# Surveying and combining the down projection's weights during the up projection, and making its token sums in two passes

## The chip, the cores and the metric

The kernel runs on one core of one Trainium2 chip. TensorE (PE) multiplies matrices; VectorE (DVE), ScalarE (ACT) and GpSimd (POOL) do the arithmetic around it; SyncE (SP) issues nearly all transfers between the chip's main memory and the on-chip buffer. The engines run at the same time, each through its own list of instructions in order, and wait for one another by semaphores.

The metric is the device time of one execution in microseconds (us), as the median of several runs. One further execution was recorded by the hardware profiler; all profile rows come from it.

## The reference

`reference()` is one layer of an encoder on x of 1024 tokens by 1024 features, in float32:

```python
h = layer_norm(x, ln_in_w, ln_in_b)
h = layer_norm(A * h + hybrid_mixer(h, ...), ln1_w, ln1_b)   # mLSTM heads and neighbourhood attention
h = layer_norm(A * h + memory_xattn(h, mem, ...), ln2_w, ln2_b)
h = layer_norm(A * h + conv_ffn(h, ...), ln3_w, ln3_b)

def conv_ffn(x, w_up, b_up, w_dw, b_dw, w_down, b_down):
    h = x @ w_up + b_up
    h = depthwise_conv3(h, w_dw) + b_dw        # along the positions
    g, u = jnp.split(h, 2, axis=-1)
    y = jax.nn.gelu(g, approximate=False) * u
    return y @ w_down + b_down
```

A is 2 to the power 0.25. The inner width is 2816, so `w_up` is 1024 x 5632 and `w_down` 2816 x 1024. The mixer begins with one combined projection of the normed x.

## The kernel before

**Arithmetic.** A float32 operand is scaled by a power of two and split into two float16 parts, a high one on ACT and a low one on DVE (`split16`, lines L204 and L205). A product then takes three matmuls (`mm3`, L225 to L227), typically of 128x512 results. To scale an operand its largest magnitude must be bounded first. That is a "survey": ACT takes absolute values and accumulates a sum for each partition.

**Seven products.** The large projections use a Strassen-like scheme. Both operands are cut into 2 x 2 blocks, and seven block products replace eight. On the weight side this needs sums of blocks, T1 to T4; on the token side S1 to S4.

**Stages.** (1) Input norm, keys and values of the memory tokens, token-major projections. (2) The feature-major part of the mixer's projection in four units u = 0..3 (`units_gen`, bank `cu` in the profile). `cu_prep` loads a unit's weights in two transfers (L459, tile `wraw`), surveys them (L311), splits them (L204, L205) and lets POOL make four sums (L477 to L480), which are split too. ACT and DVE take the results out of the banks (L506, L504). (3) mLSTM, neighbourhood attention, output projection, cross attention. (4) The up projection: a loop over v = 0..21, in which PE multiplies unit v, POOL makes the four sums of unit v + 2 (L1600 to L1603), ACT and DVE do the convolution and the gate of unit v - 1 (L1741 to L1750), and the activation y of each unit is stored to main memory. (5) The down projection. Blocks 0 to 15 of the inner width take the seven products in the order A11·B11, A12·B21, A22·T4, n2·T2, n1·T1, s3·T3, n4·B22; blocks 16 to 21 are multiplied directly. The layer norm ends it.

**The parts that the change touches.** While stage 2 runs, `td_gen` (L983 to L1008) goes through the first 16 blocks of `w_down` in 16 pieces of 512 KB. For each it loads the piece (L991, tile `draw`, three buffers), surveys it on ACT (L999, tile `djunk`), makes four 128x256 sums in place on POOL (L1001 to L1004) and stores the four combinations T1 to T4 to main memory (L1006, tensor `td`). The loop over stage 2's yields takes a step of `td_gen` at most of its turns, and an anchor (`taken`) keeps each survey behind the latest bank that ACT emptied. The other six blocks of `w_down` are surveyed one at a time in the up loop at v = 2..7 (`survey_down`, tile `sv`, two buffers, L1786).

In stage 5 `b_form` loads a weight form in two halves of 1 MB and splits it, and `a_sums(i)` loads two blocks of y (2 x 512 KB) and makes both sums that two products need: two on DVE (L1819, L1820), two on POOL (L1821, L1822), then two splits of 128x1024. The first (index m = 0, tiles SX1 and SX2 in `dx` and `zw` products) feeds n1 and n2, the second (m = 1) feeds s3 and n4. All these loads rotate through three 1 MB buffers, named `two` and `ur` in the profile.

**What sets the order.** A scheduler orders each engine's instructions from the program; `tc.issue_after` anchors hold one behind another. Every SP transfer waits in SP's list until its buffer is free, and holds up the transfers behind it.

## Time and profile before

| | us |
|---|---|
| runs | 1484.5, 1489.22, 1488.21 |
| median | 1488.21 |
| the profiled execution's own time | 1485.82 |
| its span in the profile | 1483.4 |
| PE busy | 1420.7 (96%) |
| DVE busy | 1074.7 (72%) |
| ACT busy | 850.9 (57%) |
| POOL busy | 655.3 (44%) |

The mean granted TensorE clock was 0.985 of full speed. The span is the time between the first and the last recorded instruction; the execution's own time is 2.4 us longer. Busy time counts arithmetic only. With PE busy for 96% of the span, the time can fall only where PE stands still, runs at a lower clock, or gets fewer matmuls; the stretches where that happens are found by cutting the span into windows and by asking what ended PE's waits.

Views used below: the waits (engine, what it was about to run, whom it waited for: total us, times, longest us); the windows (start and end, length, then busy us and instruction count of PE, of its weight loads, of DVE, ACT and POOL, then the granted clock, the busy share of the transfer engines, GB/s); the timeline (start us, duration us, engine, line, operation, output and input, count, and in brackets the idle time before it and what ended it); and a tile's own instructions (nanoseconds minimum/median/maximum, then first and last start).

### The profile page before, as it was taken

Reading aid. Unit: us, or ns where it says so; the run is one execution under the profiler, and the core shown is the slowest. Engines: PE = TensorE matmul, PEld = TensorE weight load, DVE = VectorE, ACT = ScalarE, POOL = GpSimd, SP = SyncE. Lnnn points to the kernel's source line nnn. Section 1 sums busy time; section 2 is a strip of 40 time slices with the busy share of each in tenths; the row PEclk is TensorE's granted clock in tenths of the full one; section 3 lists DMA queues with packets and bytes.
Section 4 is the critical chain, followed back from the end, with each engine's and each line's share of the span. In section 5 each row is a group of like instructions: output and inputs, shape, how many; then the busy total and the mean of one; then the engine's idle time right before and its main releaser. Section 6 shows DMA issues by size and latency. Waiting matters only on the chain. (4 is left out here: it accounts for less than half of the span.)

```text
span 1483.4 us, 21399 instructions
## 1 busy us (share of the span) xinstructions
PE 1420.7 (96%) x7864; PEld 835.2 (56%) x7864; DVE 1074.7 (72%) x1956; ACT 850.9 (57%) x1399; POOL 655.3 (44%) x528
## 2 busy tenths in 40 slices
PE   7999899969999999999999999999999999998997
PEld 6898777435676677675444444444444444443443
DVE  7767866733667777858756878888888778898346
ACT  4775464766564467723455667777667767645201
POOL 4444338755432675416302334454444420055494
PEclk9999999989999999999999999999999999999999
DMA  9764654467654563464452423322222225766322
GB/s 328 272 240 139 198 185 158 154 207 234 179 149 121 169 225 122 161 236 123 87 118 66 150 80 129 141 100 85 86 86 85 85 86 180 273 235 238 110 72 99
DMA packets 133040, 229.56 MB, mean 155 GB/s; under 512 B 41028, under 2 KB 86340, under 8 KB 128199
## 3 DMA queue, kind: packets, MB, share of 16 engines
q1 hardware_dynamic: 132640, 227.44, 46.1%
q8 instruction: 61, 1.00, 0.3%
q0 software_dynamic: 144, 0.49, 0.2%
q14 instruction: 45, 0.36, 0.1%
q10 hardware_dynamic: 150, 0.27, 0.0%
HBM read 166.73 MB, written 53.54 MB: 148 GB/s over the span
## 5 line engine op out<-in xcount | busy, mean ns | idle before, releaser
L225 PEld LDWEIGHTS <-whi 128*128 128x128 f16 x574 | 56.5, 98 | 68.8 <-ACT whi L204 8.7
L1742 DVE SCALAR_TENSOR_TENSOR cbuf<-C,wdw,cbuf 128x1024 f32<-128x1024 f32 x44 | 65.2, 1483 | 36.9 <-ACT cbuf L1741 36.7
L226 PEld LDWEIGHTS <-whi 128*128 128x128 f16 x574 | 56.5, 98 | 62.5 <-issue 7.2
L227 PEld LDWEIGHTS <-wlo 128*128 128x128 f16 x574 | 56.4, 98 | 61.7 <-DVE wlo L205 2.0
L1600 POOL TENSOR_TENSOR wraw<-two 128x512 f32<-128x512 f32 x15 | 30.1, 2008 | 123.0 <-issue 121.8
L205 DVE SCALAR_TENSOR_TENSOR wlo<-wraw,us,whi 128x1024 f16<-128x1024 f32 (+1 forms) x48 | 62.4, 1320 | 25.6 <-ACT whi L204 25.5
L1741 ACT ACTIVATE cbuf<-C,bdw,wdw 128x1024 f32<-128x1024 f32 x44 | 54.4, 1238 | 43.1 <-DVE C L1779 42.5
L245 POOL TENSOR_TENSOR lnrs<-lnrs,mhalf 128x1 f32<-128x1 f32 x32 | 21.2, 663 | 125.7 <-DVE lnrs L244 117.1
L1743 DVE SCALAR_TENSOR_TENSOR cbuf<-C,wdw,cbuf 128x1024 f32<-128x1024 f32 x44 | 71.3, 1621 | 1.1
L204 ACT ACTIVATE whi<-wraw,us 128x1024 f16<-128x1024 f32 (+1 forms) x48 | 51.1, 1103 | 10.8 <-DVE us L177 10.3
L225 PE MATMUL tk<-whi,Bo 128*128 128x256 f16 (+1 forms) x192 | 53.7, 280 | 1.6 <-DVE stage L205 1.6
L226 PE MATMUL tk<-wlo,Be 128*128 128x256 f16 (+1 forms) x192 | 52.6, 274 | 1.5 <-DVE wlo L205 1.5
L226 PE MATMUL tk<-wlo,Bo 128*128 128x256 f16 (+1 forms) x192 | 53.7, 280 | 0.0
L227 PE MATMUL tk<-whi,Bo 128*128 128x256 f16 (+1 forms) x192 | 53.7, 280 | 0.0
L225 PE MATMUL tk<-whi,Be 128*128 128x256 f16 (+1 forms) x192 | 52.6, 274 | 0.8 <-ACT whi L204 0.5
L227 PE MATMUL tk<-whi,Be 128*128 128x256 f16 (+1 forms) x192 | 52.6, 274 | 0.0
L225 PE MATMUL S<-kq,h1T 128*128 128x512 f16 x128 | 48.6, 379 | 0.0
L226 PE MATMUL S<-kq,h1T 128*128 128x512 f16 x128 | 48.5, 379 | 0.0
L227 PE MATMUL S<-kq,h1T 128*128 128x512 f16 x128 | 48.5, 379 | 0.0
L1821 POOL TENSOR_TENSOR wraw<-two 128x512 f32<-128x512 f32 x2 | 3.8, 1885 | 97.2 <-DMA two<-y 92.5
L1270 ACT ACTIVATE P<-P,mn 128x256 f32<-128x256 f32 (+1 forms) x64 | 35.7, 558 | 16.0 <-DVE mn L1268 14.9
L255 ACT ACTIVATE D<-D,lnrs 128x1024 f32<-128x1024 f32 x5 | 6.2, 1241 | 66.2 <-DVE lnrs L254 66.2
(654 smaller groups left out, 5159.3 us busy)
## 6 DMA issues: line engine op xcount, KB each, us to landing
two<-in_w_up_dram SPq DMA_DIRECT2D x15, 1024.0 KB
y<-cbuf SPq DMA_DIRECT2D x22, 512.0 KB
draw<-in_w_dn_dram SPq DMA_DIRECT2D x16, 512.0 KB
td<-draw SPq DMA_DIRECT2D x16, 512.0 KB
ur<-in_w_up_dram SPq DMA_DIRECT2D x7, 1024.0 KB
two<-y SPq DMA_DIRECT2D x6, 1024.0 KB
two<-y SPq DMA_DIRECT2D x12, 512.0 KB
wraw<-in_w_tok_dram SPq DMA_DIRECT2D x10, 512.0 KB
```

Source lines behind the costliest of these rows:

```text
L204: A.activation(hi, src, AF.Copy, scale=s)
L205: return V.scalar_tensor_tensor(lo, src, s, hi, op0=OP.mult, op1=OP.subtract)
L225: T.matmul(ps, lh, rh, start=first, stop=False, skip_group_check=skip)
L226: T.matmul(ps, lh, rl, start=False, stop=False, skip_group_check=skip)
L227: return T.matmul(ps, ll, rh, start=False, stop=last, skip_group_check=skip)
L245: G.tensor_tensor(rs[:, 0:1], rs[:, 0:1], mhalf[:, 0:1], OP.pow)
L255: A.activation(r, r, AF.Identity, scale=rs[:, 0:1], bias=rs[:, 1:2])
L1270: A.activation(P[:, :nk], P[:, :nk], AF.Exp, scale=-1.0, bias=mn[:, 0:1], accum_out=mn[:, 1:2])
L1600: G.tensor_tensor(S1, A21, A22, OP.add)
L1741: A.activation(c, C[:, 1:SEQ + 1], AF.Identity, scale=wdw[:, 1, j:j + 1], bias=bdw[:, j:j + 1])
L1742: V.scalar_tensor_tensor(c, C[:, 0:SEQ], wdw[:, 0, j:j + 1], c, op0=OP.mult, op1=OP.add)
L1743: V.scalar_tensor_tensor(c, C[:, 2:SEQ + 2], wdw[:, 2, j:j + 1], c, op0=OP.mult, op1=OP.add)
```

## The change

`td_gen` and its pool are removed, and with it all that stood in stage 2 for it. `survey_down` now covers all 22 blocks, from v = 2 to v = 19, one per unit and two at v = 4, 8, 12 and 16. For the first 16 it also makes the four sums on POOL, in place in `sv`, and POOL itself issues the store to `td`. The survey writes its absolute values to a scratch tile, so that `sv` keeps the weights.

The weights are laid out anew in main memory: each of 16 pieces holds the four 256-column blocks that are combined, 4 KB per partition, and `td` has the same shape. `b_form` reads every form by one access pattern of 1 KB runs.

`a_sums(m, i)` makes only one of the two sums: two additions on DVE for m = 0, three for m = 1, then one split. Each y block is so loaded twice. POOL's sixteen additions go. All eight steps with m = 0 precede the T1 form; those with m = 1 are spread behind T3 and the n1·T1 product. The final norm's vectors are loaded and scaled later.

```diff
-    td_d = dscratch("td", [4, 128, 8 * 512])
+    td_d = dscratch("td", [16, 128, D])
...
-            dp = cm.enter_context(tc.tile_pool(name="dp", bufs=1, reuse_waits="tile"))
-            def td_gen():
-
-                junk = dp.tile([128, 1024], BF, name="djunk")
-                raws = {}
-
-                def load(n):
-                    if n < 16:
-                        raws[n] = dp.tile([128, 4, 256], F32, name="draw", tag="draw", bufs=3)
-                        S.dma_start(raws[n], I["w_dn"][n // 2].rearrange("p (b c) -> p b c", b=4)[
-                            :, :, n % 2 * 256:n % 2 * 256 + 256])
-
-                load(0)
-                load(1)
-                for n in range(16):
-                    raw = raws.pop(n)
-                    with tc.issue_after(taken[0].ins):
-                        A.activation(junk, raw.rearrange("p b c -> p (b c)"), AF.Abs, accum_out=sums[:, NFF + n:NFF + n + 1])
-                    B11, B12, B21, B22 = (raw[:, i] for i in range(4))
-                    G.tensor_tensor(B11, B11, B12, OP.add)
-                    G.tensor_tensor(B12, B12, B22, OP.add)
-                    G.tensor_tensor(B22, B22, B11, OP.add)
-                    G.tensor_tensor(B21, B21, B22, OP.add)
-                    o = n // 2 * 512 + n % 2 * 256
-                    S.dma_start(td_d[:, :, o:o + 256].rearrange("n p c -> p n c"), raw)
-                    load(n + 2)
-                    yield
-            bg, td = back_gen(), td_gen()
+            bg = back_gen()
             for n, _ in enumerate(units_gen(cu0)):
-                if n % 7 % 2 == 0:
-                    next(td, None)
                 if n >= 14:
                     next(bg, None)
-            run(td)
             run(bg)
             prep(0)
             gram(0)
...
                 t = sv[i % 2]
                 with tc.issue_after(loaded.ins):
-                    S.dma_start(t, I["w_dr"][i // 2, :, i % 2 * 1024:i % 2 * 1024 + 1024])
-                A.activation(t, t, AF.Abs, accum_out=dsum[:, NG + i:NG + i + 1])
+                    S.dma_start(t, I["w_dn"][i] if i < NG else I["w_dr"][(i - NG) // 2, :, i % 2 * 1024:i % 2 * 1024 + 1024])
+                A.activation(junk[:, :D], t, AF.Abs, accum_out=dsum[:, i:i + 1])
+                if i < NG:
+                    B11, B12, B21, B22 = (t[:, n * 256:n * 256 + 256] for n in range(4))
+                    G.tensor_tensor(B11, B11, B12, OP.add)
+                    G.tensor_tensor(B12, B12, B22, OP.add)
+                    G.tensor_tensor(B22, B22, B11, OP.add)
+                    G.tensor_tensor(B21, B21, B22, OP.add)
+                    G.dma_start(td_d[i], t)
...
+            temps = [0]
+
+            def a_sums(m, i, s):
                 raw = raw8().rearrange("p (n t) -> p n t", n=2)
                 for n in range(2):
                     S.dma_start(raw[:, n], y_d[i + 8 * n])
                 (e, o), (e8, o8) = ((raw[:, n, :512], raw[:, n, 512:]) for n in range(2))
-                t, u = (W5[n].bitcast(F32) if i % 2 else wp.tile([128, WP], F32, name="wraw", tag="wraw", bufs=2)[:, :1024]
-                        for n in range(2))
-                t, u = (b.rearrange("p (x c) -> p x c", x=2) for b in (t, u))
-                V.tensor_tensor(t[:, 0], o, o8, OP.subtract)
-                V.tensor_tensor(t[:, 1], t[:, 0], e, OP.subtract)
-                G.tensor_tensor(u[:, 0], e, o, OP.subtract)
-                G.tensor_tensor(u[:, 1], t[:, 1], e8, OP.add)
-                for m, src in enumerate((t, u)):
-                    h = SH[m][i // 4][:, :, :, i % 4]
-                    split16(h[:, 0], h[:, 1], src, s)
+                k = temps[0] % 4
+                temps[0] += 1
+                t = W5[k // 2].bitcast(F32) if k % 2 else wp.tile([128, WP], F32, name="wraw", tag="wraw", bufs=2)[:, :1024]
+                t = t.rearrange("p (x c) -> p x c", x=2)
+                if m == 0:
+                    V.tensor_tensor(t[:, 0], o, o8, OP.subtract)
+                    V.tensor_tensor(t[:, 1], t[:, 0], e, OP.subtract)
+                else:
+                    V.tensor_tensor(t[:, 0], e, o, OP.subtract)
+                    V.tensor_tensor(t[:, 1], e8, o8, OP.subtract)
+                    V.tensor_tensor(t[:, 1], t[:, 1], t[:, 0], OP.subtract)
+                h = SH[m][i // 4][:, :, :, i % 4]
+                return split16(h[:, 0], h[:, 1], t, s)
...
                     raw = raw8()
-                    if name[0] == "B":
-                        S.dma_start(raw.rearrange("p (i c) -> p i c", i=4),
-                                    I["w_dn"][4 * q:4 * q + 4, :, n * 512:n * 512 + 512].rearrange("i p c -> p i c"))
-                    else:
-                        S.dma_start(raw, td_d[n, :, q * 2048:q * 2048 + 2048])
+                    S.dma_start(raw.rearrange("p (i c) -> p i c", i=8),
+                                (I["w_dn"] if name[0] == "B" else td_d)[8 * q:8 * q + 8, :, n * 256:n * 256 + 256].rearrange(
+                                    "i p c -> p i c"))
                     h, l = home[q]
-                    split16(h, l, raw, sd)
+                    end = split16(h, l, raw, sd)
                     BF_[name] += [(h[:, i * 512:i * 512 + 512], l[:, i * 512:i * 512 + 512]) for i in range(4)]
+                return end
...
-                if 1 < v < 8:
-                    survey_down(v - 2)
+                if 1 < v < NFF - 2:
+                    survey_down(v - 2 + min((v - 1) // 4, 4))
+                    if v % 4 == 0:
+                        survey_down(v - 1 + (v - 1) // 4)
...
             b_form("T2", kept["H0"])
             for i in range(4):
-                a_sums(i, s1)
+                a_sums(0, i, s1)
             Z4 = [bank("zw") for j in range(4)]
             dprod(Z4, A22, "T4", True)
             into(Z4, 1, 0, 1.0)
-            b_form("T1", YH)
             for i in range(4, 8):
-                a_sums(i, s1)
+                a_sums(0, i, s1)
+            lo = b_form("T1", YH)
             dprod(X4, n2, "T2", False, outer=True)
             into(X4, 0, 1, -1.0)
             b_form("T3", H1)
-            rw, rb, bd = vec(0, "ln2_w"), vec(1, "ln2_b"), vec(2, "b_down")
-            V.tensor_scalar(rw, rw, al, None, op0=OP.mult)
-            V.tensor_scalar(bd, bd, inv[:, 0:1], None, op0=OP.mult)
-            V.scalar_tensor_tensor(rb, rb, al, bd, op0=OP.mult, op1=OP.add)
-            lw = vec(2, "ln3_w")
+            for i in range(4):
+                a_sums(1, i, s1)
             W4 = [bank("zw") for j in range(4)]
             dprod(W4, n1, "T1", True, outer=True)
             into(W4, 1, 1, 1.0)
+            for i in range(4, 8):
+                a_sums(1, i, s1)
             b_form("B22", kept["H0"])
+            rw, rb, bd = vec(0, "ln2_w"), vec(1, "ln2_b"), vec(2, "b_down")
+            with tc.issue_after(lo.ins):
+                V.tensor_scalar(rw, rw, al, None, op0=OP.mult)
+                V.tensor_scalar(bd, bd, inv[:, 0:1], None, op0=OP.mult)
+                V.scalar_tensor_tensor(rb, rb, al, bd, op0=OP.mult, op1=OP.add)
+            lw = vec(2, "ln3_w")
+            dprod(X4, s3, "T3", False, outer=True)
             yq = f16(xp.tile([128, 4096], F32, name="yq", tag="X1h")).rearrange("p (m n f t) -> p m n f t", m=2, n=2, f=2)
             for m in range(2):
                 y_pair(NG + 2 * m, sy[1][1], yq[:, m, 0], yq[:, m, 1])
             y_pair(NG + 4, sy[1][1], *(t.rearrange("p (f t) -> p f t", f=2) for t in W5))
-            dprod(X4, s3, "T3", False, outer=True)
...
-    a["w_dn"] = C(np.concatenate([wd[:8], wd[8:16]], axis=2))
+    a["w_dn"] = C(wd[:16].reshape(2, 8, 128, 2, 2, 256).transpose(1, 4, 2, 0, 3, 5).reshape(16, 128, D))
```

**Stage 2, ACT and SP.** Unit 3's preparation on ACT before the change: `L999` is a survey of `td_gen`, `L204` the high half of a split, `L506` empties a bank.

```order
L506 ACTIVATE q_3220<-cu,bsc,us 128x2x128
L999 ACTIVATE djunk,sums<-draw 128x1024
L506 ACTIVATE k_3219<-cu,bsc,us 128x2x128
L506 ACTIVATE k_3221<-cu,bsc,us 128x2x128
L204 ACTIVATE whi<-wraw,us 128x512
L999 ACTIVATE djunk,sums<-draw 128x1024
L204 ACTIVATE whi<-wraw,us 128x1024
L204 ACTIVATE whi<-ev_3709,us 128x512
```

The same place after it:

```order
L506 ACTIVATE q_3220<-cu,bsc,us 128x2x128
L506 ACTIVATE k_3219<-cu,bsc,us 128x2x128
L506 ACTIVATE k_3221<-cu,bsc,us 128x2x128
L204 ACTIVATE whi<-wraw,us 128x512
L204 ACTIVATE whi<-wraw,us 128x1024
L204 ACTIVATE whi<-ev_3621,us 128x512
```

The two surveys are gone, and the two splits of the same weights now stand next to each other. SP's list for the loads of units 2 and 3 (`L459`) and what stood between them, before:

```order
L459 DMA wraw<-in_w_cu_dram 128x1024 x2
L1006 DMA td<-draw 128x4x256
L991 DMA draw<-in_w_dn_dram 128x4x256
L1006 DMA td<-draw 128x4x256 x2
L991 DMA draw<-in_w_dn_dram 128x4x256
L459 DMA wraw<-in_w_cu_dram 128x1024
L991 DMA draw<-in_w_dn_dram 128x4x256
L459 DMA wraw<-in_w_cu_dram 128x1024
```

and after:

```order
L829 DMA mo<-ev 128x256 x3
L931 DMA mo<-mo 128x512 x2
L459 DMA wraw<-in_w_cu_dram 128x1024 x4
L917 DMA whi<-mrow 128x512 x2
L949 DMA wraw<-in_w_col_dram 128x1024
```

Unit 3's two loads no longer stand behind stores and loads of `td_gen`.

**Up loop, POOL.** Before, POOL's list goes from the four sums of one unit straight to those of the next. After the change a unit with one survey reads as follows (`L1568` to `L1571` are the former L1600 to L1603):

```order
L1568 TENSOR_TENSOR wraw<-ur 128x512
L1570 TENSOR_TENSOR wraw<-ur 128x512
L1569 TENSOR_TENSOR wraw<-wraw,ur 128x512
L1571 TENSOR_TENSOR wraw<-ur,wraw 128x512
L1757 TENSOR_TENSOR sv_9052<-sv_9052 128x256
L1758 TENSOR_TENSOR sv_9052<-sv_9052 128x256
L1759 TENSOR_TENSOR sv_9052<-sv_9052 128x256
L1760 TENSOR_TENSOR sv_9052<-sv_9052 128x256
L1761 DMA td<-sv_9052 128x1024
```

Four small sums and a store were added behind the unit's own four.

**Down stage, DVE.** The token sums for n2·T2 (`SX2l` is a low half for m = 0, `SX2h` one for m = 1) before:

```order
L1819 TENSOR_TENSOR wraw<-two_12439 128x512
L1819 TENSOR_TENSOR whi<-two_12452 128x512
L1820 TENSOR_TENSOR wraw<-wraw,two_12439 128x512
L1820 TENSOR_TENSOR whi<-whi,two_12452 128x512
L205 SCALAR_TENSOR_TENSOR SX2l<-wraw,sc,SX2l 128x2x512
L205 SCALAR_TENSOR_TENSOR SX2l<-whi,sc,SX2l 128x2x512
L1819 TENSOR_TENSOR wraw<-ur 128x512
L205 SCALAR_TENSOR_TENSOR SX2h<-wraw,sc,SX2h 128x2x512
L205 SCALAR_TENSOR_TENSOR SX2h<-wlo,sc,SX2h 128x2x512
L1820 TENSOR_TENSOR wraw<-wraw,ur 128x512
L1819 TENSOR_TENSOR whi<-two_12476 128x512
```

and after:

```order
L205 SCALAR_TENSOR_TENSOR SX2l<-wraw,sc,SX2l 128x2x512
L1799 TENSOR_TENSOR wraw<-wraw,two_12407 128x512
L176 TENSOR_SCALAR sc<-sc 128x1
L1798 TENSOR_TENSOR whi<-ur 128x512
L177 TENSOR_SCALAR sc<-sc 128x1
L1958 TENSOR_SCALAR sc<-sc 128x1
L1799 TENSOR_TENSOR whi<-whi,ur 128x512
L205 SCALAR_TENSOR_TENSOR SX2l<-wraw,sc,SX2l 128x2x512
L205 SCALAR_TENSOR_TENSOR SX2l<-whi,sc,SX2l 128x2x512
L1798 TENSOR_TENSOR wlo<-two_12415 128x512
L1799 TENSOR_TENSOR wlo<-wlo,two_12415 128x512
L205 SCALAR_TENSOR_TENSOR SX2l<-wlo,sc,SX2l 128x2x512
```

The splits for m = 1 no longer stand between those for m = 0; they follow in a second pass, behind the T1 form.

More of the change, by code (lines that the diff above doesn't have):

```diff
@@ L450, in encoder @@
             V.tensor_scalar(bsc[:, 8:12], bcol[:, 8:12], -0.125, None, op0=OP.mult)
-            cu, taken = {}, [None]
+            cu = {}
             def cu_prep(u, home=None):
@@ L505, in cu_take @@
                     else:
-                        taken[0] = A.activation(dst, src, AF.Identity, scale=cu[u][1], bias=bsc[:, i:i + 1])
+                        A.activation(dst, src, AF.Identity, scale=cu[u][1], bias=bsc[:, i:i + 1])
             def units_gen(first):
@@ L1808, in s_home @@
                     "p (n x i c) -> p n x i c", n=2, x=2, i=4)
-            def a_sums(i, s):
+            temps = [0]
+            def a_sums(m, i, s):
                 raw = raw8().rearrange("p (n t) -> p n t", n=2)
```

## The prediction

> **What bounds the kernel now.** I read the busy times first, then the windows, then the waits of PE and the timeline around each.
>
> ```profile
> span 1483.4 us, 21399 instructions
> PE 1420.7 (96%) x7864; PEld 835.2 (56%) x7864; DVE 1074.7 (72%) x1956; ACT 850.9 (57%) x1399; POOL 655.3 (44%) x528
> ```
>
> PE stands still for some 63 us of the span, so those, and the stretches at a low clock, are what any change can win. The windows show where they lie.
>
> ```profile
> 0.00:50.00 50.00, 40.48 (x220) 34.12 (x221) 34.83 (x62) 25.73 (x36) 21.65 (x20) 0.90 0.86 307
> 300.00:350.00 50.00, 35.44 (x181) 19.09 (x178) 16.30 (x38) 31.44 (x71) 30.52 (x38) 0.90 0.62 199
> 950.00:1000.00 50.00, 49.72 (x232) 22.45 (x231) 43.85 (x52) 38.59 (x44) 23.15 (x13) 1.00 0.34 126
> 1000.00:1050.00 50.00, 50.00 (x235) 22.80 (x234) 41.51 (x49) 37.48 (x41) 20.59 (x11) 1.00 0.26 95
> 1009.90:1028.10 18.20, 18.20 (x87) 8.29 (x85) 14.58 (x18) 12.94 (x15) 7.88 (x4) 1.00 0.23 86
> 1300.00:1350.00 50.00, 45.65 (x212) 20.47 (x210) 46.89 (x39) 26.23 (x23) 28.10 (x16) 1.00 0.70 250
> 1350.00:1400.00 50.00, 50.00 (x233) 22.70 (x232) 30.66 (x18) 19.63 (x16) 16.91 (x6) 1.00 0.51 181
> ```
>
> In the up loop (1000 to 1050) PE never rests: 235 matmuls in 50 us, 0.213 us each. One unit of the loop is the row of 18.2 us. PE loses 14.6 us in 300 to 350, stage 2, where the clock also falls; 9.5 us at the start; 4.4 us in the down stage. Of these stretches the timeline shows what PE waited for.
>
> **The change in stage 2.** PE's longest wait in stage 2, 8.44 us (its row follows), has this on ACT behind it:
>
> ```profile
> 310.29 0.72 ACT L204 ACTIVATE whi<-wraw,us 128x512 f16<-128x512 f32 x1
> 318.18 1.06 ACT L999 ACTIVATE djunk<-draw 128x1024 bf16<-128x1024 f32 x1 [7.17 <-DMA draw<-in_w_dn_dram]
> 319.24 1.13 ACT L204 ACTIVATE whi<-wraw,us 128x1024 f16<-128x1024 f32 x1
> ```
>
> The second split of unit 3's weights was ready to run at 311: its scale is that of the first, and its data had been surveyed for it. It stood behind a survey that waited 7.17 us for a `draw` load. The survey goes, and the split follows at 311. On PE (timeline, then two windows, then the wait for the low half from the list of waits):
>
> ```profile
> 303.80 0.38 PE L225 MATMUL cu<-Bo,whi 128*128 128x512 f16 x1 [2.87 <-ACT k L506]
> 321.04 0.61 PE L225 MATMUL cu<-TX1l,whi 128*128 128x512 f16 x1 [8.44 <-ACT whi L204]
> 350.11 1.11 PE L867 MATMUL tp<-ident,k 128*128 128x128 f32 x4 [2.23 <-ACT kw L871]
> 321.00:326.00 5.00, 3.83 (x9) 1.17 (x10) 4.61 (x5) 4.98 (x14) 2.64 (x2) 0.50 0.83 231
> 351.00:356.00 5.00, 5.00 (x20) 2.03 (x18) 0.86 (x2) 3.34 (x10) 4.12 (x6) 0.74 0.48 160
> PE cu L227 <- DVE wlo L205: 1.1, 1, 1.1
> ```
>
> After the 8.44 us the granted clock was 0.50: 9 matmuls in 5.00 us, where 9 x 0.213 = 1.9 us would do; 1.1 us of the rest is the wait for wlo, 2.0 us the clock. After the 2.23 us it was 0.74: 20 matmuls in 5.00 us instead of 4.3, 0.7 us. The first wait, 2.87 us, ends with a bank emptied late (L506), because ACT had first to survey weights that SP had issued late:
>
> ```profile
> 288.47 2.92 DVE L205 SCALAR_TENSOR_TENSOR wlo<-wraw,us,whi 128x512 f16<-128x512 f32 x2 [0.73 <-ACT whi L204]
> 290.33 4.30 SPq L1006 DMA_DIRECT2D td<-draw  x2
> 295.45 0.83 SPq L459 DMA_DIRECT2D wraw<-in_w_cu_dram  x1
> 298.19 0.57 SPq L459 DMA_DIRECT2D wraw<-in_w_cu_dram  x1
> ```
>
> The last reader of the old `wraw` ended at 288.47 + 2.92 = 291.4. SP could have issued then; it held two stores of `td` and two loads of `draw` first, so the loads came 4 to 7 us late. They now stand alone in SP's list. So on the path lie 2.87 + 8.44 + 2.0 + 1.1 + 2.23 + 0.7 = 17.3 us. What stays: with unit 3's chain some 4 us earlier and PE 2.87 us earlier, the low half, which DVE makes behind the high one, stays late by 1 to 2 us, and the wait at 350 (an ACT chain in which a 1.06 us survey is one part) may shrink only by half. I take **-13 us**; at worst, with the loads no earlier and only the survey gone, 7.2 + 2.0 - 1.2 = -8 (the low half waits 1.2 as before); at best -17.
>
> **At the start.** Three of the loads of `draw` were issued ahead of weights that the first products need:
>
> ```profile
> 13.01 3.04 SPq L991 DMA_DIRECT2D draw<-in_w_dn_dram  x3
> 20.10 1.72 SPq L572 DMA_DIRECT2D wr<-in_w_xk_dram  x3
> 30.48 0.58 PE L227 MATMUL mem<-memTh,wlo 128*128 128x256 f32 x1 [3.49 <-DVE wlo L578]
> ```
>
> They are 1.5 MB, 4.9 us at the window's 307 GB/s, and the wait of 3.49 us hangs on a weight behind them. The scheduler reorders this stage too, which may cost something. I take **-3 us**, from +1 (other weights late, nothing won) to -8 (most of the 9.5 us).
>
> **In the up loop** each new survey adds a load, 1.24 us on ACT, four POOL additions and a POOL-issued store, 16 times in 13 units. PE hides all of it as long as every engine stays under 18.2 us a unit. The rows for the old surveys, the additions, the only POOL-issued transfer, the unit's POOL and DVE work and the slack of ACT:
>
> ```profile
> L1786 ACT ACTIVATE sv<-sv x6: 1041/1057/1057, 884.5 to 964.1; 128x1024 f32<-128x1024 f32 x6
> L1001 POOL TENSOR_TENSOR draw<-draw x16: 713/724/1705, 274.7 to 373.2; 128x256 f32<-128x256 f32 x16
> L1162 POOL DMA_DIRECT2D vec<-in_na_mask_dram x1: 757/757/757, 398.9 to 398.9; - x1
> 1014.32 2.24 POOL L1601 TENSOR_TENSOR wraw<-wraw,ur 128x512 f32<-128x512 f32 x1
> 1016.64 1.27 POOL L1603 TENSOR_TENSOR wraw<-ur,wraw 128x512 f32<-128x512 f32 x1
> 1028.13 2.19 POOL L1600 TENSOR_TENSOR wraw<-two 128x512 f32<-128x512 f32 x1 [10.23 <-issue]
> 1013.26 2.17 DVE L1743 SCALAR_TENSOR_TENSOR cbuf<-C,wdw,cbuf 128x1024 f32<-128x1024 f32 x1
> 1019.64 1.28 DVE L1743 SCALAR_TENSOR_TENSOR cbuf<-C,wdw,cbuf 128x1024 f32<-128x1024 f32 x1
> 1017.04 1.24 ACT L1741 ACTIVATE cbuf<-C,bdw,wdw 128x1024 f32<-128x1024 f32 x1 [2.86 <-DVE C L1779]
> ```
>
> POOL: 4 x 0.72 + 0.76 = 3.7 us for a survey, at the contended 1.7 us some 7.6, in a gap of 10.23; two surveys in a unit fit at 7.4 and not quite at 15. ACT: 12.94 + 1.24 of 18.2, and it stands idle for 2.86 us in one piece. DVE: its additions stretch from 1.28 to 2.17 us while POOL runs. In this unit POOL's 7.88 us stretched DVE by about 1.2 us; 2.9 more, at that rate, add 0.4, at the worst row's rate (0.89 us of stretch in 2.17 us) 1.2. So 14.6 becomes 15 to 16, or up to 17 in the four double units: under 18.2. The old surveys ran until 964, and PE lost 0.28 us in 950 to 1000. I take **+0.5 us**, from 0 to +6: if POOL took 1.7 us throughout, a double unit would need 7.9 + 15.2 = 23 us of POOL, 5 over, of which the unit behind it can give back 18.2 - 15.5 = 2.7; some 1.5 us would come through, four times.
>
> The Trainium skill (SBUF — State Buffer, "Who interferes with whom") says that a VectorE instruction with two SBUF inputs and a GpSimd instruction that reads SBUF contend for one port pair, and that the loser is blocked for the whole instruction. The rows agree in kind (2.17 against 1.28, 2.24 against 1.27), but both were lengthened there, by 0.9 us each, which is less than a full block of 2.2. By that rule the time would be that of rival (1).
>
> **In the down stage** PE lost time to the token sums:
>
> ```profile
> 1341.90 0.39 PE L227 MATMUL dx<-whi,SX2l 128*128 128x512 f16 x1 [2.18 <-DVE SX2l L205]
> 1346.37 0.39 PE L227 MATMUL dx<-whi,SX2l 128*128 128x512 f16 x1 [1.71 <-DVE SX2l L205]
> 1293.46 0.92 DVE L1819 TENSOR_TENSOR wraw<-two 128x512 f32<-128x512 f32 x1 [0.16 <-DMA two<-y]
> 1309.41 0.68 DVE L1819 TENSOR_TENSOR whi<-two 128x512 f32<-128x512 f32 x1
> 1337.21 1.76 DVE L1819 TENSOR_TENSOR whi<-two 128x512 f32<-128x512 f32 x1
> 1340.57 1.27 DVE L205 SCALAR_TENSOR_TENSOR SX2l<-wraw,sc,SX2l 128x1024 f16<-128x1024 f32 x1
> ```
>
> A block's m = 0 work on DVE, two additions beside POOL's (up to 1.76 us each) and two splits, becomes 2 x 0.68 + 1.27 = 2.6 us with POOL silent, and T1's loads and splits no longer stand in the middle. The first block is there at 1293; eight at 250 GB/s (1300 to 1350) take 33 us, so the last sum is done by about 1329. PE took the last block at 1346.37, which is 1342 without the waits: 2.18 + 1.71 = 3.9 us go. The second pass costs 3 x 0.68 + 1.27 = 3.3 us a block, 26.5 us, on a DVE that was busy for 30.66 of 50 us in 1350 to 1400 and has given work away. T1 and half of T3, 3 MB, come before it, so it begins about 1342. Product s3·T3 needs its first block when n2·T2 (1344.6: ten matmuls after 1346.37, less 3.9) and n1·T1 (96 matmuls, 20.4 us) are done, at 1365, and from then one in 2.6 us (12 matmuls). The 8 MB loaded again are the risk (rival 3). I take **-4 us**, from -4.4 (all that the window 1300 to 1350 lost) to +5 (a second pass that slips by two blocks).
>
> **The sum** against the profiled execution's 1485.82 us: -13 - 3 + 0.5 - 4 = -19.5, so 1466.3. That execution lies 2.4 us under the median of the runs, so I put the time at **1467 us**, between the two.
>
> **Rivals.** (1) *The up loop becomes bound by DVE.* If every new POOL addition blocks DVE for its whole 0.72 us, 64 x 0.72 = 46 us come in 13 units, 3.5 us a unit. DVE's 41.51 of 50 us are 15.1 a unit, and 43.85 are 16.0: 18.6 to 19.5 against 18.2, times 13 is 5 to 17 us. Time 1471 to 1483; I say 1474, near the lower row, which is the later one. For it: the lengthened rows. Against: both engines lost only 0.9 us in a shared stretch. (2) *Another chain ends last in stage 2.* Unit 3's weights still need load, survey, scale, split; if ACT and DVE reach them no earlier, only half of the 13 is won: 1473; if the mixer behind it waits for something else as well, 1480. Against: ACT and POOL lose 1.24 and 2.9 us of work a piece there. (3) *Slower: the second pass over y makes the down stage wait for transfers.* From about 1291 to 1385 (1365 and the 20.4 us of s3·T3), when n4·B22 begins, SP must bring 8 MB of y, T1, T3, 8 MB of y again and B22: 22 loads of 1 MB, 23 MB in 94 us, 245 GB/s. The row 1300 to 1350 moved 250 at a busy share of 0.70, so the engines could give 250 / 0.70 = 357; but 1350 to 1400 moved 181 at 0.51. If three buffers hold the rate at 181, the 23 MB take 127 us, 33 us too long, and the time is 1499. It decides against the change where the rate stays below some 200 GB/s (115 us, 21 over). Against: the 181 were paced by what PE consumed, PE was at 50.00 of 50. (4) *It does not do what it says*, since all work merely changed places and PE finds other waits of the same length: 1485.
>
> **Chances.** Forecast 0.62, (1) 0.14, (2) 0.13, (3) 0.05, (4) 0.06. A difference under 0.3% (4.5 us) can't be told from none here. Faster: forecast, (1), nearly all of (2): 0.88; same: (4) and the rest of (2), 0.07; slower: (3), 0.05. The range runs from 1457 (the best end of stage 2 and the start together) to 1481 (rivals 1 and 2 with little left).
>
> **What would show it.** In stage 2 no wait of PE on `whi` over 2 us, the clock near 1.0 in 300 to 350, PE near 48 of 50. At the start less than 9.5 us idle. In the up loop units of 18.2 us and PE at 50.00; a DVE row near 50 busy would be rival 1. In the down stage no wait on SX2l, and none on the m = 1 tiles; a wait on loads of y or of B22 would be rival 3. The forecast is wrong if stage 2 is shorter by less than 8 us, or if any later stage takes back more than 5 us.

## The result, and the profile after

The changed kernel takes 1464.52 us (median of 6 runs, 1460.16 to 1468.6); the kernel before, run beside it, 1488.72 us (6 runs, 1484.5 to 1490.63). The ratio is 0.9842, with a 95% interval of 0.9817 to 0.9867. The forecast was 1467 us. The profiled execution took 1465.71 us, 20.1 us less than that of before; the sum of the prediction had said 1466.3, 19.5 us less. The medians lie further apart, by 24.2 us, because the profiled execution of before was 2.9 us under its median and that of the changed kernel 1.2 us over its own.

The total is nearly met, its terms are not. The table cuts each profiled execution at matmuls that both kernels have: the first and last into a bank `cu` (stage 2), into `z` (up loop), the last into `dn` (the direct blocks that end the down stage), and the end of the span.

| us | before | after | difference | predicted |
|---|---|---|---|---|
| start to first `cu` | 261.98 | 255.58 | -6.4 | -3 |
| stage 2 | 104.75 | 86.88 | -17.9 | -13 |
| stage 2 to first `z` | 486.65 | 484.97 | -1.7 | none |
| up loop | 417.71 | 422.76 | +5.0 | +0.5 |
| last `z` to last `dn` | 201.97 | 197.11 | -4.9 | -4 |
| last matmul to end of span | 10.4 | 16.7 | +6.3 | none |

The busy times and the windows of the changed kernel that answer to those shown of before (in a window row: width, then busy time and number of instructions of PE, PEld, DVE, ACT and POOL, then granted clock, DMA share and GB/s):

```profile
span 1464.0 us, 21447 instructions
PE 1413.5 (97%) x7864; PEld 832.2 (57%) x7864; DVE 1093.4 (75%) x1980; ACT 852.4 (58%) x1399; POOL 670.7 (46%) x528
```

```profile
0.00:50.00 50.00, 42.51 (x255) 36.56 (x256) 40.21 (x72) 30.63 (x42) 24.26 (x22) 0.93 0.76 280
50.00:100.00 50.00, 50.00 (x442) 45.88 (x440) 41.77 (x77) 37.82 (x47) 23.78 (x12) 1.00 0.81 303
300.00:350.00 50.00, 49.13 (x283) 29.79 (x282) 23.62 (x67) 33.85 (x88) 6.74 (x8) 1.00 0.33 88
900.00:950.00 50.00, 44.81 (x209) 20.13 (x208) 42.45 (x40) 34.87 (x44) 41.90 (x32) 1.00 0.40 151
1000.00:1050.00 50.00, 50.00 (x236) 22.75 (x234) 44.70 (x48) 39.68 (x46) 42.06 (x31) 1.00 0.45 162
1250.00:1300.00 50.00, 50.00 (x234) 22.92 (x233) 43.63 (x47) 29.06 (x27) 0.00 (x0) 1.00 0.92 322
1300.00:1350.00 50.00, 50.00 (x234) 22.64 (x232) 44.79 (x42) 25.20 (x23) 9.25 (x3) 1.00 0.88 327
```

Two windows of before to compare with, which were not shown yet:

```profile
50.00:100.00 50.00, 47.99 (x419) 44.04 (x418) 41.10 (x81) 40.20 (x49) 21.07 (x12) 1.00 0.81 305
900.00:950.00 50.00, 50.00 (x235) 22.77 (x234) 41.20 (x47) 39.09 (x45) 21.50 (x12) 1.00 0.32 117
```

Four things are to be seen. In 300 to 350 PE is busy for 49.13 us where it had 35.44, at a clock of 1.00 where it had 0.90: from its first to its last `cu` PE stood still for 16.3 us before and for 2.5 us after. In the up loop's steady part (1000 to 1050) PE is as full as before although POOL's work doubled, from 20.59 to 42.06 us. The up loop's loss lies in one window, 900 to 950, where PE does 209 matmuls instead of 235. And the stretches that load the activations twice moved 322 and 327 GB/s with PE at 50.00.

The last `dx` matmul of s3·T3, the reading of its bank, and the end, before (timelines of PE, DVE and POOL):

```profile
1389.76 0.38 PE L227 MATMUL dx<-whi,SX2h 128*128 128x512 f16 x1
1390.58 2.48 DVE L1959 TENSOR_TENSOR D<-D,dx 128x512 f32<-128x512 f32 x4
1391.94 4.69 POOL L2012 TENSOR_TENSOR D<-D,wraw 128x1024 f32<-128x1024 f32 x2 [30.21 <-DVE D L1959]
1441.50 5.65 POOL L2012 TENSOR_TENSOR D<-D,wraw 128x1024 f32<-128x1024 f32 x2
1472.79 0.27 PE L227 MATMUL dn<-whi,wlo 128*128 128x256 f16 x1
```

and after:

```profile
1363.99 0.38 PE L227 MATMUL dx<-whi,SX2h 128*128 128x512 f16 x1
1365.75 2.35 DVE L205 SCALAR_TENSOR_TENSOR BY<-ur,sc,BY 128x2048 f16<-128x2048 f32 x1 [4.57 <-ACT BY L204]
1368.02 2.35 DVE L205 SCALAR_TENSOR_TENSOR wlo<-two,sc,whi 128x2048 f16<-128x2048 f32 x1
1370.28 2.47 DVE L1940 TENSOR_TENSOR D<-D,dx 128x512 f32<-128x512 f32 x4
1371.70 4.69 POOL L1998 TENSOR_TENSOR D<-D,wraw 128x1024 f32<-128x1024 f32 x2 [14.94 <-DVE D L1940]
1422.40 5.66 POOL L1998 TENSOR_TENSOR D<-D,wraw 128x1024 f32<-128x1024 f32 x2
1447.02 0.27 PE L227 MATMUL dn<-whi,wlo 128*128 128x256 f16 x1
```

Before, DVE began to empty the banks (`into`, L1959) 0.4 us after the end of PE's last matmul of this product. After the change it has two splits of the next weights ahead of that (L205), the first of which waits 4.57 us, and begins 5.9 us after it. POOL's residual chain (from the first to the last `D` += `wraw`) needs the result, and starts 7.3 us after that matmul instead of 1.8.

The end of the span follows this chain. From the end of its last addition to the end of the span it is 36.3 us before (1447.15 to 1483.4) and 36.0 after (1428.06 to 1464.0), and it is 35.9 to 36.8 us in every other kernel below that leaves these additions on POOL. The chain itself lasts 55.2 us before and 56.4 after. From the last `dx` matmul to the last `dn` PE needs 82.9 us in both. So of the 6.3 us 5.5 are the late start and 1.1 the longer chain, less 0.3 behind it.

### The profile page after: what moved, and what is told of

The parts are those of the page before. It is cut to its first block, busy times and chain, and to the rows that moved or that the text cites. A ratio compares the mean times of both kernels' runs of the same rounds, so it can differ in the third digit from the quotient of the medians.

```text
span 1464.0 us, 21447 instructions
## 1 busy us (share of the span) xinstructions
PE 1413.5 (97%) x7864; PEld 832.2 (57%) x7864; DVE 1093.4 (75%) x1980; ACT 852.4 (58%) x1399; POOL 670.7 (46%) x528
## 5 line engine op out<-in xcount | busy, mean ns | idle before, releaser
L1996 POOL TENSOR_TENSOR wraw<-wraw,vec 128x1024 f32<-128x1024 f32 x8 | 22.3, 2797 | 166.5 <-DMA wraw<-h 166.5
L1710 DVE SCALAR_TENSOR_TENSOR cbuf<-C,wdw,cbuf 128x1024 f32<-128x1024 f32 x44 | 71.5, 1626 | 35.5 <-ACT cbuf L1709 35.5
L205 DVE SCALAR_TENSOR_TENSOR wlo<-wraw,us,whi 128x1024 f16<-128x1024 f32 (+1 forms) x48 | 63.8, 1348 | 20.3 <-ACT whi L204 20.3
L1711 DVE SCALAR_TENSOR_TENSOR cbuf<-C,wdw,cbuf 128x1024 f32<-128x1024 f32 x44 | 76.6, 1743 | 1.1
L204 ACT ACTIVATE whi<-wraw,us 128x1024 f16<-128x1024 f32 (+1 forms) x48 | 51.1, 1103 | 15.2 <-DVE us L177 14.6
L1568 POOL TENSOR_TENSOR wraw<-two 128x512 f32<-128x512 f32 x15 | 29.6, 1973 | 59.9 <-issue 29.9
L922 POOL TENSOR_SCALAR_AFFINE_SELECT whi<-whi 128x512 f32<-128x512 f32 x16 | 10.2, 640 | 83.1 <-ACT whi L919 73.6
```

What stands on the lines that cost most here:

```text
L204: A.activation(hi, src, AF.Copy, scale=s)
L205: return V.scalar_tensor_tensor(lo, src, s, hi, op0=OP.mult, op1=OP.subtract)
L922: G.affine_select(E, E, pattern=[[0, 4], [s_, 128]], compare_op=OP.is_ge, fill=0.0, base=0, channel_multiplier=-s_)
L1568: G.tensor_tensor(S1, A21, A22, OP.add)
L1710: V.scalar_tensor_tensor(c, C[:, 0:SEQ], wdw[:, 0, j:j + 1], c, op0=OP.mult, op1=OP.add)
L1711: V.scalar_tensor_tensor(c, C[:, 2:SEQ + 2], wdw[:, 2, j:j + 1], c, op0=OP.mult, op1=OP.add)
```

## The experiments

Shares are against the kernel before, run on the same chip in the same session; times are medians in us.

### Which half of the change gives the gain

The first keeps the changed kernel's surveys in the up loop, and puts the token sums and the order of the down stage back as they were; the second does the opposite.

```diff
-            def a_sums(m, i, s):          # after: two passes, all on VectorE
+            def a_sums(i, s):             # as before: one pass, m = 1 partly on GpSimd
...
-            for i in range(4):
-                a_sums(1, i, s1)          # after: second pass, behind the T3 form
```

> The weight half of the change alone: surveys and sums of the weights in the up loop, the new layout, but the token sums and their order as before. Two theories on the token half. Theory A (it wins on TensorE and loses as much at the end): in the changed kernel's trace the last matmul came 25.8 us earlier but the end only 19.4, so the token half is worth -4.9 + 6.4 = +1.5 us, and this kernel should take about 1464 us, the same as the changed one, with some 10 us between the last matmul and the end as before. Theory B (the token half is worth its 4 us and the late end comes from elsewhere): about 1468 to 1469 us. On both, stage 2 and the start are shorter by 24 us and the up loop longer by 5.

> The token half alone: two passes of token sums on VectorE, the weights surveyed and combined in the mixer as before. Theory A: the last matmul some 4 to 5 us earlier, the end later behind it by about 6 us, so 1488 to 1491 us, no gain. Theory B: 1484 us. If the second pass over y made the stage wait for transfers, TensorE would show waits in the down stage and the time would be above 1495.

The weight half alone: 1462.56 us, ratio 0.9856 (0.9833 to 0.9879). The token half alone: 1483.19 us, 0.9994 (0.9979 to 1.0009). So the surveys' move is the whole gain; the token half is worth nothing that can be measured. Stage 2 takes 86.2 us with the weight half alone and 101.8 with the token half alone. The latter has stage 2 as before (104.75), so a difference of 3 us between two profiles of this stage says nothing. In the profile of the second run last `z` to last `dn` does shrink, from 201.97 to 197.11 us, and the end behind the last matmul grows from 10.4 to 13.7: most of what PE won is given back behind it.

### The end behind the last matmul

The next two put the splits of the next weights behind the emptying of the banks: first two of the three, then also the third.

```diff
-            into(X4, 1, 1, OP.subtract)
-            for m in range(2):
-                w_pair(m, *YH[m])
+            drained = into(X4, 1, 1, OP.subtract)     # now returns its last instruction
+            with tc.issue_after(drained.ins):
+                for m in range(2):
+                    w_pair(m, *YH[m])
...
-            w_pair(2, *H1[0])                         # second run only:
+            with tc.issue_after(drained.ins):
+                w_pair(2, *H1[0])
```

> The changed kernel with one order altered: two of the three weight splits for the direct blocks stand on VectorE behind the eight additions that empty the banks of the fourth product, not ahead of them. In the changed kernel these additions began 5.9 us after the product's last matmul (0.4 us before the change), and GpSimd's residual chain, which starts on them, ended 19.1 us earlier instead of 25. If this delay is what the end pays, the time falls by 5 to 6 us, to about 1459, and the end lies some 10 to 12 us behind the last matmul. If GpSimd's chain is bound by its loads of the residual, or by its own work, nothing changes: 1464.

> The changed kernel with all three weight splits of the direct blocks behind the additions that empty the fourth product's banks. In the run before this one (two of the three moved) the third still stood ahead of them, waiting 10.4 us for its high half, and they began 5.7 us after the product's last matmul, as in the changed kernel. With all three behind, they should begin within 0.5 us of it. If the late start of GpSimd's residual chain is what the end pays, the end comes some 5 us earlier, at 10 to 12 us behind the last matmul: 1459 us. If GpSimd's chain is paced by its own 24 additions and its loads wherever it starts, less than 2 us: 1463.

With two splits moved: 1464.75 us, 0.9872 (0.9854 to 0.989), no gain. The timeline of DVE says why: the third split still stood ahead, so DVE began to empty the banks 5.7 us after PE's last matmul of the product, against 5.9.

```profile
1364.79 2.35 DVE L205 SCALAR_TENSOR_TENSOR wlo<-two,sc,whi 128x2048 f16<-128x2048 f32 x1 [10.43 <-ACT whi L204]
1367.06 2.47 DVE L1940 TENSOR_TENSOR D<-D,dx 128x512 f32<-128x512 f32 x4
```

With all three moved (1460.23 us, 0.9838, 0.9817 to 0.9858) DVE empties the banks at 1364.19, while PE is still at the last of them, and the end behind the last matmul shrinks from 16.7 to 12.5 us. That is 4.2 us in the profile; the time as a whole can't be told from that of the change. It is not back to 10.4: the residual chain starts 7.8 us sooner relative to PE, but lasts 59.9 us instead of 56.4. POOL's residual operations now run beside the splits on DVE, and those beside them are longer (timelines of PE, DVE and POOL):

```profile
1364.19 2.48 DVE L1940 TENSOR_TENSOR D<-D,dx 128x512 f32<-128x512 f32 x4 [5.09 <-PE dx L227]
1365.71 0.38 PE L227 MATMUL dx<-whi,SX2h 128*128 128x512 f16 x1
1371.55 7.47 POOL L1997 TENSOR_TENSOR wraw<-wraw,vec 128x1024 f32<-128x1024 f32 x2 [1.24 <-DMA wraw<-h]
1372.38 4.43 DVE L205 SCALAR_TENSOR_TENSOR BY<-ur,sc,BY 128x2048 f16<-128x2048 f32 x1
1378.98 6.70 POOL L1998 TENSOR_TENSOR wraw<-wraw,vec 128x1024 f32<-128x1024 f32 x2
```

7.47 and 6.70 us, where the same form takes 4.66 us in a run shown below, and 4.43 us for the split, which takes 2.35 in the rows of the change above.

### The 5 us of the up loop

Two edits of the changed kernel: one leaves out the 64 GpSimd additions (the weights then stay uncombined, so the down projection isn't computed; loads, surveys and stores stay), one takes the six blocks that need no addition first.

```diff
-                    G.tensor_tensor(B11, B11, B12, OP.add)     # one run: these four left out
-                    G.tensor_tensor(B12, B12, B22, OP.add)
-                    G.tensor_tensor(B22, B22, B11, OP.add)
-                    G.tensor_tensor(B21, B21, B22, OP.add)
...
-                    survey_down(v - 2 + min((v - 1) // 4, 4))  # the other run
+                    survey_down((v - 2 + min((v - 1) // 4, 4) + NG) % NFF)
                     if v % 4 == 0:
-                        survey_down(v - 1 + (v - 1) // 4)
+                        survey_down((v - 1 + (v - 1) // 4 + NG) % NFF)
```

> The changed kernel without the 64 GpSimd additions behind the surveys (the combined weights are left uncombined, so the down projection's values are not computed; loads, surveys, stores and all splits stay). If GpSimd's additions cost the up loop its 5 us by slowing VectorE, the loop lasts 417 to 418 us from its first to its last matmul, as before the change, against 422.8. If the cost comes from the surveys on ScalarE or the added transfers, it stays near 422.

> The changed kernel with the six surveys that need no sums (the direct blocks) put first in the up loop, and the sixteen with GpSimd sums behind them. TensorE waited 5.5 us in the units v = 3 to 5 of the changed kernel, where VectorE instructions took up to 4.87 us instead of 1.28 beside GpSimd's sums. If the first units are special (the loop has no lead yet), the waits go: about 1460 us. If any double unit with sums pays them, they move to a later unit and the time stays at 1464.

Without the additions the up loop takes 417.42 us (1457.47 us in all, one run); before it took 417.71, after 422.76. So the 5 us are the additions' alone, not the loads, surveys or stores. With the additions begun later the loop takes 417.49 us, with all 64 of them in it (1457.19 us, 0.9822, 0.9801 to 0.9842). So they cost nothing but in the loop's first units. They stand in v = 2 to 14 in the changed kernel, and in v = 7 to 19 with the plain blocks first. PE's waits in the first of these units in the changed kernel, from its timeline:

```profile
918.55 0.38 PE L225 MATMUL z<-TX1l,unitYh 128*128 128x512 f16 x1 [1.91 <-ACT C L1739]
937.77 0.38 PE L225 MATMUL z<-TX1l,whi 128*128 128x512 f16 x1 [0.88 <-ACT C L1739]
945.30 0.23 PE L183 MATMUL mx<-identb,am 128*128 128x128 bf16 x1 [2.41 <-DVE am L1546]
```

Together they are 5.2 us. The first stands in a unit with one survey, whose DVE work beside the additions ran late: the pair of L1711 in the first row below took 3.96 us, and 2.47 in the run without additions. The other waits stand in and behind the first unit with two surveys. The remaining rows are POOL and DVE ahead of the longest wait:

```profile
906.00 3.96 DVE L1711 SCALAR_TENSOR_TENSOR cbuf<-C,wdw,cbuf 128x1024 f32<-128x1024 f32 x2
933.19 3.91 POOL L1760 TENSOR_TENSOR sv<-sv 128x256 f32<-128x256 f32 x2
938.16 1.29 POOL L1568 TENSOR_TENSOR wraw<-ur 128x512 f32<-128x512 f32 x1
939.41 1.27 POOL L1570 TENSOR_TENSOR wraw<-ur 128x512 f32<-128x512 f32 x1
940.63 1.26 POOL L1569 TENSOR_TENSOR wraw<-wraw,ur 128x512 f32<-128x512 f32 x1
938.11 4.87 DVE L1710 SCALAR_TENSOR_TENSOR cbuf<-C,wdw,cbuf 128x1024 f32<-128x1024 f32 x1
943.01 2.17 DVE L1711 SCALAR_TENSOR_TENSOR cbuf<-C,wdw,cbuf 128x1024 f32<-128x1024 f32 x1
945.10 0.14 DVE L1546 CAST am<-l 128x1 bf16<-128x1 f32 x1
```

The second row is the last pair of the eight additions of the two surveys; the next unit's own sums follow without a pause. DVE's L1710 then took 4.87 us, 3.6 more than the 1.28 of its shortest, while POOL did three sums in 1.29 + 1.27 + 1.26 = 3.8 us. `am` stands behind it in DVE's queue, and PE waited 2.41 us for that. In the groups of the same instruction (minimum, median and maximum in ns) the changed kernel, which comes first, has such a row alone; the second group is without the additions, the third with the plain blocks first:

```profile
L1710 DVE SCALAR_TENSOR_TENSOR cbuf<-C,wdw,cbuf x39: 1277/1533/4872, 882.1 to 1228.9; 128x1024 f32<-128x1024 f32 x39
```

```profile
L1710 DVE SCALAR_TENSOR_TENSOR cbuf<-C,wdw,cbuf x40: 1276/1526/2290, 881.4 to 1234.9; 128x1024 f32<-128x1024 f32 x40
```

```profile
L1710 DVE SCALAR_TENSOR_TENSOR cbuf<-C,wdw,cbuf x40: 1271/1530/2292, 879.7 to 1233.2; 128x1024 f32<-128x1024 f32 x40
```

The same holds for the other kernels here: a row of 4.85 to 4.87 us stands in each that has the additions on POOL from v = 2 on, and none above 2.31 in any other.

That the first units are hit and later double units are not may be because the loop has no lead yet; no run shows it.

Would the additions be better on DVE?

```diff
-                    G.tensor_tensor(B11, B11, B12, OP.add)     # and the three behind it
+                    V.tensor_tensor(B11, B11, B12, OP.add)
```

> The changed kernel with the 64 additions behind the surveys on VectorE and not on GpSimd. Without them the loop lasted 417.4 us, with them on GpSimd 422.8. If the cost is the two engines stretching each other, the additions on VectorE (some 0.35 us each, half of a 128x512 one at 0.68) cost 1.4 us a survey in units where VectorE has 3 us to spare: 417 to 419 us for the loop, about 1460 us in all. If VectorE's work is the limit whichever engine adds, 422 or more, 1464 or above.

No: 1477.7 us, 0.9962 (0.9942 to 0.9981), and an up loop of 439.55 us, 16.8 more than with the additions on POOL. One addition is shorter there, 0.41 us at its shortest against 0.72 on POOL, but PE stood still for 20.2 us of the loop, against 8.1 (the first and the last addition of a survey, as groups, and the loop's beginning as a window):

```profile
L1757 DVE TENSOR_TENSOR sv<-sv x16: 409/837/1497, 885.5 to 1120.6; 128x256 f32<-128x256 f32 x16
L1760 DVE TENSOR_TENSOR sv<-sv x16: 404/410/425, 891.4 to 1128.0; 128x256 f32<-128x256 f32 x16
900.00:1000.00 100.00, 90.42 (x406) 39.94 (x405) 84.38 (x109) 69.86 (x84) 38.29 (x28) 0.97 0.39 144
```

DVE was busy for 84.38 of these 100 us, no larger a share than in the change (44.70 of 50). So it was not full; that the additions' places in its list made other work late is likely and not shown.

### Both mends together, and without the token half

The first of these takes the plain blocks first and moves all three splits; the second adds to it that DVE instead of GpSimd adds the residual to `C`; the third is the weight half alone with the plain blocks first.

```diff
-                G.tensor_tensor(C[tt], C[tt], r, OP.add)       # second run only
+                V.tensor_tensor(C[tt], C[tt], r, OP.add)
```

> The changed kernel with both altered orders: the six plain surveys first in the up loop, and the fourth product's banks emptied ahead of all three weight splits. If the two causes are independent, 5.5 us from the up loop and 5 from the end: about 1453 us, ratio to the kernel before 0.977. If the end is paced by GpSimd alone: 1458.

> The kernel with both altered orders, and the eight residual additions at the end (128x1024 each) done by VectorE and not by GpSimd. In the run with both orders GpSimd's residual chain took 59.8 us from the first of these additions to the last, eight of them 18.6 us, and the end lay 12.4 us behind the last matmul (10.3 before the change). If GpSimd's chain sets the end, it is over some 10 us earlier and the end lies about 10 us behind the last matmul: 1451 us. If the norms of the last tiles on VectorE set it, whose turn gets longer by 1.3 us a tile, no change or up to 5 us more: 1454 to 1458.

> The weight half alone, with the six plain surveys first: what the token half is worth beside it. The weight half alone took 1462.6 us; the plain surveys first are worth 5.4 us (the loop from 422.8 to 417.5), so 1457 us. The kernel with both altered orders and the token half took 1453.8 us. So theory A, that the token half wins 4 us only once the banks are emptied first: this run at 1457, 3 us slower than that one. If it is worth nothing even then, 1454.

1453.82 us, 0.9798 (0.9777 to 0.9818; runs 1451.81 to 1457.28); 1454.46 us, 0.9802 (0.9774 to 0.9831); 1455.96 us, 0.9806 (0.9778 to 0.9835). The first has the lowest median of this study, but the three can't be told apart. The runs of the kernel with only the splits moved, timed beside the first, lie above all of its own (1459.77 to 1463.31), so the other order of the blocks is worth some 6 us. The residual additions on DVE change nothing (12.8 us behind the last matmul, against 12.4): POOL then waits longer for loads of `h` ahead of its pairs, 4.71, 4.67 and 3.22 us, against 0.7 to 1.3 with the additions on POOL.

```profile
1379.46 4.66 POOL L1997 TENSOR_TENSOR wraw<-wraw,vec 128x1024 f32<-128x1024 f32 x2 [4.71 <-DMA wraw<-h]
```

That two `wraw` buffers are the cause is likely and wasn't tried. Without the token half the time can't be told from that with it, mended or not. In the profiles of the mended kernels the stretch to the last `dn` is 5.8 us longer (202.86 against 197.11) and the end 2.4 us shorter (9.9 against 12.4).

### The start, and stage 2

Two edits of the kernel before. One anchors the loads of `draw` behind a load of stage 2's weights, which takes the first three out of the start; the other lets GpSimd issue the stores of `td`, meant to let SP issue the late loads of `wraw` sooner.

```diff
-                        S.dma_start(raws[n], I["w_dn"][n // 2].rearrange(
+                        with tc.issue_after(held[0].ins):      # one run
+                            S.dma_start(raws[n], I["w_dn"][n // 2].rearrange(
...
-                    S.dma_start(td_d[:, :, o:o + 256].rearrange("n p c -> p n c"), raw)
+                    G.dma_start(td_d[:, :, o:o + 256].rearrange("n p c -> p n c"), raw)   # the other
```

> The kernel before the change with one alteration: the first three loads of the mixer's weight surveys wait in SP's list behind the second unit's loads of stage 2, and so leave the start (they were issued at 13 us). If the 6.4 us that the changed kernel won ahead of stage 2 come from these 1.5 MB, the first matmul of stage 2 starts at 255 to 257 us, against 261.98. If they come from the scheduler's other order at the start, it stays at 260 to 262. Stage 2 itself may get longer, since the loads come late there.

> The kernel before the change, with the stores of the combined weights in the mixer issued by GpSimd and not by SP; loads, surveys and sums stay. SP then no longer waits for GpSimd's sums ahead of unit 3's loads. If SP's list made unit 3's loads late, the wait of 2.87 us on the emptied bank goes, and stage 2 lasts 98 to 101 us from its first to its last matmul, not 104.75; what is left of the 8.44 us, a survey on ScalarE that waits for its load, should still be seen. If stage 2 is long because of the work of the surveys and sums, it stays at 103 to 105.

Without the early loads the first `cu` comes at 253.17 us, 8.8 us sooner: those 1.5 MB account for all that the change won there (it came at 255.58). In all the kernels without early loads it comes at 251.7 to 255.6, in all those with them at 261.6 to 262.0. Yet the whole won only about 6 us (1479.44, one run): stage 2 took 101.36 us, and the mixer behind it 6.0 us more. The 3.49 us wait didn't go in the change; its row has the same length and another releaser:

```profile
30.34 0.58 PE L227 MATMUL mem<-memTh,wlo 128*128 128x256 f32 x1 [3.49 <-DVE lnrs L244]
```

With the stores off SP the 2.87 us wait went, and that on `whi` fell from 8.44 to 1.0, but stage 2 took 103.06 us, against 104.75, and the kernel 1494.4 us (one run). The edit did not do what it was meant to: unit 3's two loads were issued from 295.34 on, against 295.45 and 298.19 before, since two loads of `draw` still held SP ahead of them. SP's timeline, and the waits between 240 and 400 us (who waited and for what, then the sum, the number and the longest):

```profile
285.00 10.26 SPq L991 DMA_DIRECT2D draw<-in_w_dn_dram  x2
295.34 1.06 SPq L459 DMA_DIRECT2D wraw<-in_w_cu_dram  x2
```

```profile
ACT djunk L999 <- DMA draw<-in_w_dn_dram: 22.2, 7, 5.8
PE num L1041 <- ACT hm L1053: 6.8, 1, 6.8
PE tp L867 <- ACT kw L871: 3.0, 1, 3.0
PE stb L878 <- ACT kw L871: 2.5, 1, 2.5
PE cu L227 <- DVE wlo L205: 2.0, 1, 2.0
PE cu L225 <- ACT whi L204: 1.0, 1, 1.0
```

The surveys, still there, held ACT for 22.2 us in seven waits for loads, and PE waited at other places: `tp`, `stb` and `wlo` in stage 2, `num` behind it. So the two waits could shrink without stage 2 getting shorter by more than profiles of it differ. How stage 2's gain divides between SP's order and the work of the surveys and sums stays open; that both together make it is shown by the two halves of the change.

## Why the prediction was right in sum, and where not

**Stage 2** (-13, best -17): -17.9. Of these 13.7 us are waits of PE and 4.1 are time in its matmuls, for which the sum had 2.7 us of low clock; the clock is now 1.00. Every wait that it named went but for 0.8 us on the low half, the one of 2.23 us at 350 too, which I had only halved. The chain reading was right and its size too careful: I took unit 3's low half to stay late by 1 to 2 us. The rival of another chain in stage 2 did not occur there. In the run with the stores off SP, where the surveys stayed and unit 3's loads came no sooner, PE did wait on other chains.

**The start** (-3): -6.4. Right in its cause, the early loads of `draw`, and undersized, with one wrong step: that the 3.49 us wait hung on a weight behind them. That wait stayed, also in the run that held only those loads back. Ahead of the first `cu` PE's other waits fell by 4.0 us in sum, by 2.0 in 0 to 50 (40.48 to 42.51 us busy) and by 2.0 in 50 to 100 (47.99 to 50.00); the other 2.4 us are shorter matmuls, with the clock in 0 to 50 at 0.93 instead of 0.90.

**The up loop** (+0.5, from 0 to +6): +5.0. The size lies inside the bounds; its step failed twice. I worked with the shared stretch, both engines lengthened by 0.9 us, and the decisive row is one DVE instruction stopped over three GpSimd sums that were not lengthened (1.27 us, as in the prediction's shorter row). The Trainium skill (SBUF — State Buffer, "Who interferes with whom") has the loser of the shared port blocked while the other works; this row agrees with it, at 3.6 us for 3.8 us of sums, where the rows of the prediction's profile had only part of a block. And my upper bound let 1.5 us come through in each of four units with two surveys. Only three of them have additions (v = 4, 8 and 12; at v = 16 both surveys are plain). 3.3 us came through at the first of them, 1.9 in a unit with a single survey ahead of it, and nothing later. Rival 1, DVE as the bound of all 13 units, did not come: DVE was at 44.70 of 50 us with PE at 50.00.

**The down stage** (-4, at best -4.4): -4.9 as far as PE goes. No wait on `SX2l` or on the m = 1 tiles is left. The transfers that rival 3 feared ran at 322 and 327 GB/s at shares of 0.92 and 0.88, which make 350 and 372 at a full share, near the 357 that I worked out from 250 at 0.70; it did not occur.

**What the sum lacked** is the end behind the last matmul, +6.3 us. I ended the down stage at PE and said that DVE "has given work away"; it had a second pass and splits ahead of the emptying of a bank, on which POOL's residual chain and then the last layer norm hang. The down stage as a whole, with its end, is +1.5 us by the profile, and the runs say that the token half is worth nothing. The forecast named as its own condition of failure that a later stage takes back more than 5 us; this end did, and so, barely, did the loop. That the total came out is luck: 8 us more than forecast won in stage 2 and at the start, 1.7 in the mixer and 0.9 by PE in the down stage stand against 11 us lost in the loop and at the end that the sum did not have.

## What to carry to other kernels

A transfer of work that frees an engine in a tight stage pays by that stage's waits, and these are read well from what stood ahead of the late instruction in its queue. Before a run that alters a queue is taken as a test of that reading, look whether the late instruction came sooner in it. A gain on the bounding engine counts only as far as the last instruction of the program: follow what empties its last bank, and who waits for that, before a term for the last stage is put into the sum. Where two engines lengthen each other's work, try the new work of one in later units as well: the same 64 additions cost 5 us from v = 2 on and nothing from v = 7 on. Read the maximum of a group's durations beside its median.

## What the hardware did that was not expected

One VectorE instruction was stopped for 3.6 us over three GpSimd sums in a row (4.87 instead of 1.28 us), and those sums took 1.26 to 1.29 us each. In other units of the same loop both engines were lengthened instead (GpSimd up to 2.31, VectorE to 2.29), and in the run with all splits moved GpSimd's residual products took 7.47 us a pair instead of 4.66. What decides between the two is open.

The addition of two 128x256 tiles took 0.41 us on VectorE and 0.72 on GpSimd where nothing lengthened it, and the loop was 16.8 us longer with all 64 on VectorE. The Trainium skill (GPSIMD Engine Reference, section 4.1) sends such additions to VectorE; the durations agree with it, the time of this kernel does not.
